# One weight sum of the first MLP set formed by adding DMAs instead of vector adds, in a one-core decoder block

## The chip, the cores and the metric

The kernel runs on one core of one Trainium2 chip. The metric is the device time of one execution in microseconds (us), the median over runs; lower is better. All data is float32.

## What is computed

One decoder block on 512 tokens of width 1024: a mixer, a cross-attention, and a squared-ReLU MLP, each behind an RMSNorm and with a residual add, and a final RMSNorm. The change lies in the first projection of the MLP:

```python
hm = rms_norm(x, g_mlp[l])
x = x + jnp.square(jax.nn.relu(hm @ w_up[l])) @ w_down[l]   # w_up 1024 x 4096, w_down 4096 x 1024
return rms_norm(x, g_final)
```

## The kernel before

**Tiling.** Everything stands transposed: features on the 128 partitions, 512 tokens along the free axis. A product of float32 matrices is made of three matmuls (`mm3`, lines 105 to 107): both operands are split into a rounded high part (a cast on ACT, line 111) and a low remainder (a subtraction on DVE, line 112), and hi·hi, hi·lo and lo·hi are summed in PSUM. A weight block is a tile of 128 x 1024; it is loaded to `wraw` (3 buffers) or `mraw` (5 buffers), split into `whi`/`wlo` (3 buffers each) or, for two of five blocks of the MLP, into two tiles of `mhl` (4 buffers), and consumed by TensorE in the order in which the program lists the blocks.

**The up projection.** It is done in 8 sets of 512 output features, two sets for each of 4 groups, each followed by that group's 8 down blocks. A set multiplies a 2 x 2 arrangement of weight blocks A11, A12, A21, A22 with a 2 x 2 arrangement of the normed input by seven block products instead of eight: three of them use A11, A12 and A22, and four use sums of blocks, s1 = A22 + A21, s3 = A21 + A11, s2 = s1 + A11 and s4 = s2 + A12. The right factors of the seven (B11, T1, B21, T2, T3, T4, B22) are sums of scaled residual tiles, made once in `right_factors` and `right_rest` (lines 756 to 796). In the first set the order is A11, s1, A12, s2, s3, A22, s4, in the others A11, A12, s1, s2, s3, A22, s4.

**How sums are formed.** `load` (line 155) fetches s1 and s3: a plain DMA of the first block on SP's queue into an `mraw` tile, then a DMA of the second block on POOL's queue that adds to the tile (line 164). s2 and s4 have no load: `combined` (line 175) adds A11, and later A12, in place into the tile of s1 with a DVE add (line 179). So the tile of s1 holds s1, then s2, then s4, and A11 and A12 stay in their buffers until they have been added.

**Order.** `weights` (line 205) is called before each block product: it loads the blocks up to seven ahead and prepares (combines and splits) those up to four ahead. TensorE's order is that of the program (manual schedule). The order on ACT, DVE, POOL and SP is written when the program is built, by a list scheduler with a timeline model of its own; on the chip each of these engines runs its list in order, and a waiting instruction holds all behind it. The tiles of `mraw` and `mhl` take the memory of an earlier pool and exist only from `renew` on, inside the projection before the MLP (`co`, the output projection of the cross-attention, 8 blocks in the order 0, 4, 1, 5, 2, 6, 3, 7). Its last block is consumed directly before A11 of the first set. When a `co` block m is done, `done_co` adds the residual (line 572), and makes the right factors of feature block m: for m < 4 two scaled copies on ACT (lines 764, 765), a difference on DVE (line 766) and the split into a `mix` tile, which is B11 and T1 of that block; for m of 4 to 7 the other factors.

```python
RIGHT = {"A11": "B11", "s2": "T2", "s1": "T1", "s3": "T3", "A12": "B21", "A22": "T4", "s4": "B22"}
def block_product(w, rhs, o):
    for i in range(2):
        for k in range(4):
            e = slice((4 * i + k) * P, (4 * i + k + 1) * P)
            mm3(o[:, i * M:(i + 1) * M], w[0][:, e], w[1][:, e], *rhs[k], k == 0, k == 3)
```

Of the kernel before, what the change touches and what calls it, by code (L numbers as in the profile page):

```python
# [14 lines left out]
ALU = mybir.AluOpType  # L15
# [35 lines left out]
def block_kernel(ctx: ExitStack, tc: tile.TileContext, x0g, xT, memT, wv, wm, wst, wckv, wpool, vecs, csts, outT):  # L51
    nc = tc.nc
# [9 lines left out]
            name=nc.get_next_instruction_name(), act_func_set_id=6, ins=[], outs=[],  # L62
# [13 lines left out]
    def sb(tag, shape, bufs, dt=F32):  # L76
        p = apool if tag in EARLY_TAGS else late["pool"] if tag in LATE_TAGS else pool
        return p.tile(shape, dt, tag=tag, name=nm(tag), bufs=bufs)
# [16 lines left out]
    def f(ap):  # L95
        return ap.bitcast(F32)
# [13 lines left out]
    def split(hi, lo, src, eng=V):  # L110
        S.copy(hi, src)  # L111
        eng.tensor_tensor(lo, src, f(hi), op=ALU.subtract)  # L112
# [25 lines left out]
    blocks = []  # L138
# [5 lines left out]
    raw, ready = {}, {}  # L144

    def fetch(key, src, tag, bufs):
        if key not in raw:
            raw[key] = sb(tag, [P, D], bufs)
            nc.sync.dma_start(raw[key], src)
        return raw[key]  # L150

    def part(n, name):
        return wst[4 * n + PARTS.index(name)]

    def load(i):
        if i >= len(blocks):
            return
        if isinstance(blocks[i], tuple):
            n, name = blocks[i]
            if name in ("s1", "s3"):  # L160
                first, then = ("A22", "A21") if name == "s1" else ("A21", "A11")
                if (n, name) not in raw:
                    r = fetch((n, name), part(n, first), "mraw", 5)
                    nc.gpsimd.dma_start(r, part(n, then), accum_op=ALU.add)  # L164
            elif name in PARTS:
                fetch((n, name), part(n, name), "mraw" if name == "A11" else "wraw", 5 if name == "A11" else 3)
        elif i < 2 and i not in raw:
            r = raw[i] = sb("wraw", [P, D], 3)
            nc.sync.dma_start(r[:, :T], blocks[i][:, :T])
            load_x(2 * i + 1)  # L170
            nc.sync.dma_start(r[:, T:], blocks[i][:, T:])
        else:
            fetch(i, blocks[i], "wraw", 3)

    def combined(n, name):

        if name in ("s2", "s4"):
            r = raw[n, "s1"]
            V.tensor_tensor(r, r, raw[n, "A11" if name == "s2" else "A12"], op=ALU.add)
            return r  # L180
        return raw[n, name]

    def prep(i):
        if i >= len(blocks) or i in ready:
            return
        load(i)
        r = combined(*blocks[i]) if isinstance(blocks[i], tuple) else raw[i]
        if i >= FIRST_UP and i % 5 > 2:
            hi = sb("mhl", [P, D], 4, F32R)
            lo = sb("mhl", [P, D], 4, F32R)  # L190
        else:
            hi = sb("whi", [P, D], 3, F32R)
            lo = sb("wlo", [P, D], 3, F32R)
        if i == 0:
            V.tensor_copy(hi[:, :T], r[:, :T])
            V.tensor_tensor(lo[:, :T], r[:, :T], f(hi[:, :T]), op=ALU.subtract)
            split(hi[:, T:], lo[:, T:], r[:, T:])
        elif i == 1:
            for c in (slice(T), slice(T, D)):
                split(hi[:, c], lo[:, c], r[:, c])  # L200
        else:
            split(hi, lo, r, G if i in WPOOL else V)
        ready[i] = (hi, lo)

    def weights(i):
        far = 4 if i >= FIRST_UP else 0
        for j in range(i, i + 4 + far):
            if j < FIRST_UP or late:
                load(j)
        for j in range(i, i + 3 + far // 2):  # L210
            if j < FIRST_UP or late:
                prep(j)
        return ready.pop(i)
# [123 lines left out]
    def load_x(k):  # L337
        xr[k] = tmp()
        nc.sync.dma_start(xr[k], xT[:, k, :])

    def x_in(k):
        pr = pair("xg", 8)
        scaled(pr[:, 0, :], pr[:, 1, :], xr[k], vec[:, G_MIX + k:G_MIX + k + 1])
        xg[k] = (pr[:, 0, :], pr[:, 1, :])

    load(0)
    x_in(0)
    prep(0)
    x_in(1)
    load_x(2)  # L350
# [679 lines left out]
```

## Time and profile before

| | us |
|---|---|
| median of 3 runs (lowest to highest) | 723.29 (722.18 to 724.42) |
| the profiled execution, its own time | 722.57 |
| its span in the profile | 720.8 |
| TensorE busy in the span | 706.5 (98%) |
| VectorE (DVE) / ScalarE (ACT) busy | 510.6 (71%) / 392.5 (54%) |

The profile is of one execution. The span runs from its first to its last instruction; 1.8 us of its own time lie around it. All times in the rows below are us from the span's start, durations of single instructions by group are ns where it says so. An idle time in brackets names what released the engine; where an engine waited for several things, the last is named. SP and POOL issue DMAs: q1 is the queue of the plain loads issued on SP, q0 that of the adding loads issued on POOL. TensorE's granted clock was 1.00 in every stretch up to 620 us.

### The profile page before, as it was taken

The page shows a single profiled execution, that of the slowest core. Times are in us where ns is not written, and L with a number is a line of the kernel's source. Part 1 is how long each engine was busy: PE and PEld are TensorE (multiplying, and loading weights), DVE is VectorE, ACT ScalarE, POOL GpSimd, SP SyncE. Part 2 cuts the span into 40 slices and gives each one's busy share as a digit, 9 for nine tenths or more (in the row PEclk, how much of TensorE's full clock was granted, in tenths as well). Part 3 has the DMA queues.
Part 4 walks back from the last instruction along what each step waited for, and adds up shares of the span by engine and source line. Part 5 has one row for each costly group of instructions (what it writes and reads, how often), then busy time and mean ns, then how long its engine had stood idle before and what let it go on. Part 6 is the DMA issues. An engine that isn't in the chain of part 4 may idle for free.

```text
span 720.8 us, 10378 instructions
## 1 busy us (share of the span) xinstructions
PE 706.5 (98%) x4016; PEld 617.0 (86%) x4016; DVE 510.6 (71%) x797; ACT 392.5 (54%) x646; POOL 66.9 (9%) x59
## 2 busy tenths in 40 slices
PE   8999999999999999999999999999999999999995
PEld 6887888788889888888879988999889988899894
DVE  7698999975888546572999954598446973589525
ACT  7498998676766434452865641355214641256432
POOL 0044112534000000000000000000000000000000
PEclk9999999999999999999999999999999999999999
DMA  8443223143525552113924850558216661305103
GB/s 315 151 118 116 88 75 116 60 146 119 176 88 176 181 170 83 65 58 143 246 79 127 237 164 30 150 111 294 89 33 167 205 182 58 88 30 161 45 1 116
DMA packets 28257, 91.09 MB, mean 126 GB/s; under 512 B 3089, under 2 KB 5137, under 8 KB 28209
## 3 DMA queue, kind: packets, MB, share of 16 engines
q1 hardware_dynamic: 25856, 81.92, 33.5%
q0 software_dynamic: 2352, 8.52, 7.0%
q8 instruction: 31, 0.51, 0.3%
q14 instruction: 18, 0.14, 0.1%
HBM read 86.24 MB, written 2.10 MB: 123 GB/s over the span
## 4 chain that ended last, share of the span: by engine, by line
PE 89%; DVE 5%; ACT 4%; issue 1%; DMA 0%; POOL 0%; DVEq 0%; SPq 0%; ACTq 0%
PE acc L105 17%; PE acc L106 17%; PE acc L107 17%; PE sc L105 11%; PE sc L106 11%; PE sc L107 11%; ACT tmp L447 1%; PE sc L386 1%; PE sc L388 1%; PE sc L390 1%; DVE tmp L445 1%; DVE wlo L112 1%; ACT tmp L417 1%; ACT whi L111 1%; DMA wraw<-wv 0%
## 5 line engine op out<-in xcount | busy, mean ns | idle before, releaser
L111 ACT CAST whi<-wraw 128x1024 fp32r<-128x1024 f32 (+1 forms) x94 | 97.2, 1035 | 107.5 <-PE acc L106 41.0
L105 PE MATMUL acc<-xg,whi 128*128 128x512 f32 x392 | 155.0, 395 | 0.0
L107 PE MATMUL acc<-xg,wlo 128*128 128x512 f32 x392 | 153.0, 390 | 0.0
L106 PE MATMUL acc<-xg,whi 128*128 128x512 f32 x392 | 152.7, 390 | 0.0
L112 DVE TENSOR_TENSOR wlo<-wraw,whi 128x1024 fp32r<-128x1024 f32 (+1 forms) x94 | 115.1, 1226 | 26.8 <-ACT whi L111 26.4
L107 PEld LDWEIGHTS acc<-xg,wlo 128*128 128x128 f32 x392 | 73.6, 188 | 15.8
L105 PEld LDWEIGHTS acc<-xg,whi 128*128 128x128 f32 x392 | 73.7, 188 | 14.5
L106 PEld LDWEIGHTS acc<-xg,whi 128*128 128x128 f32 x392 | 73.7, 188 | 14.3
L572 DVE TENSOR_TENSOR vr<-acc,vr 128x512 f32<-128x512 f32 x39 | 26.9, 690 | 76.5 <-PE acc L107 76.4
L105 PE MATMUL sc<-mix,whi 128*128 128x256 f32 (+1 forms) x184 | 54.2, 295 | 0.0
L107 PE MATMUL sc<-mix,wlo 128*128 128x256 f32 (+1 forms) x184 | 54.1, 294 | 0.0
L106 PE MATMUL sc<-mix,whi 128*128 128x256 f32 (+1 forms) x184 | 54.0, 294 | 0.0
L164 POOL DMA_DIRECT2D mraw<-wst x16 | 13.8, 864 | 429.1 <-DMA mraw<-wst 302.3
L111 ACT CAST whi<-mraw 128x1024 fp32r<-128x1024 f32 x24 | 25.0, 1052 | 45.9 <-PE acc L106 33.0
L890 DVE TENSOR_TENSOR tmp<-sc,tmp 128x512 f32<-128x512 f32 x56 | 37.5, 684 | 6.5 <-PE sc L107 6.4
L111 ACT CAST mhl<-wraw 128x1024 fp32r<-128x1024 f32 x19 | 20.0, 1052 | 34.4 <-PE acc L106 18.0
L106 PE MATMUL acc<-xg,mhl 128*128 128x512 f32 x96 | 37.4, 390 | 0.0
L105 PE MATMUL acc<-xg,mhl 128*128 128x512 f32 x96 | 37.4, 389 | 0.0
L107 PE MATMUL acc<-xg,mhl 128*128 128x512 f32 x96 | 37.4, 389 | 0.0
L107 PEld LDWEIGHTS sc<-mix,wlo 128*128 128x128 f32 x184 | 34.5, 188 | 1.1
L105 PEld LDWEIGHTS sc<-mix,whi 128*128 128x128 f32 x184 | 34.6, 188 | 1.0
L106 PEld LDWEIGHTS sc<-mix,whi 128*128 128x128 f32 x184 | 34.5, 187 | 1.1
(274 smaller groups left out, 1731.4 us busy)
## 6 DMA issues: line engine op xcount, KB each, us to landing
wraw<-wm SPq DMA_DIRECT2D x76, 512.0 KB, 3.5
mraw<-wst SPq DMA_DIRECT2D x24, 512.0 KB, 3.9
wraw<-wckv SPq DMA_DIRECT2D x16, 512.0 KB, 3.4
mraw<-wst POOLq DMA_DIRECT2D x16, 512.0 KB, 6.1
wraw<-wst SPq DMA_DIRECT2D x16, 512.0 KB, 3.4
s<-s SPq DMA_DIRECT2D x8, 256.0 KB, 3.7
vr<-xT SPq DMA_DIRECT2D x8, 256.0 KB, 4.5
outT<-mix SPq DMA_DIRECT2D x8, 256.0 KB, 2.4
```

The source lines that it names most:

```text
L105: nc.tensor.matmul(o, lh, rh, start=start, stop=False)
L106: nc.tensor.matmul(o, lh, rl, start=False, stop=False)
L107: nc.tensor.matmul(o, ll, rh, start=False, stop=stop)
L111: S.copy(hi, src)
L112: eng.tensor_tensor(lo, src, f(hi), op=ALU.subtract)
L164: nc.gpsimd.dma_start(r, part(n, then), accum_op=ALU.add)
L386: nc.tensor.matmul(o[i], xg[k][0][:, tb], wh[:, c], start=k == 0, stop=False)
L388: nc.tensor.matmul(o[i], xg[k][1][:, tb], wh[:, c], start=False, stop=False)
L390: nc.tensor.matmul(o[i], xg[k][0][:, tb], wl[:, c], start=False, stop=k == KC - 1)
L417: S.copy(b[32 * (j ^ 1):32 * (j ^ 1) + 32, :], o[32 * j:32 * j + 32, :])
L572: V.tensor_tensor(t, o, t, op=ALU.add)
L890: V.tensor_tensor(u[new], o, u[old], op=ALU.add)
```

## The change

For the first set alone (n = 0), s2 gets an `mraw` tile of its own, loaded together with s1: a plain DMA of A22, then an adding DMA of A21 and an adding DMA of A11. `combined` returns this tile for s2 and for s4 without an add. Right behind the split of s2 a third adding DMA puts A12 into the same tile, which makes it s4. The two DVE adds of line 179 are gone for this set; the other seven sets are as they were, and `mraw` keeps its five buffers.

```diff
@@ load
                 if (n, name) not in raw:
                     r = fetch((n, name), part(n, first), "mraw", 5)
                     nc.gpsimd.dma_start(r, part(n, then), accum_op=ALU.add)
+                if (n, name) == (0, "s1") and (n, "s2") not in raw:
+                    r = fetch((n, "s2"), part(n, first), "mraw", 5)
+                    for then in "A21", "A11":
+                        nc.gpsimd.dma_start(r, part(n, then), accum_op=ALU.add)
@@ combined
+        if name in ("s2", "s4") and n == 0:
+            return raw[n, "s2"]
         if name in ("s2", "s4"):
             r = raw[n, "s1"]
             V.tensor_tensor(r, r, raw[n, "A11" if name == "s2" else "A12"], op=ALU.add)
@@ prep
         ready[i] = (hi, lo)
+        if blocks[i] == (0, "s2"):
+            nc.gpsimd.dma_start(r, part(0, "A12"), accum_op=ALU.add)
```

## Rows read from the trace of the kernel before

**Rows 1.** The page, busy time in us, share of the span, instructions, by engine (DVE is VectorE, ACT is ScalarE).
```profile
PE 706.5 (98%) x4016; PEld 617.0 (86%) x4016; DVE 510.6 (71%) x797; ACT 392.5 (54%) x646; POOL 66.9 (9%) x59
```

**Rows 2.** Busy time of each engine by stretch: the stretch, its length, busy us and instructions of each engine, TensorE's granted clock, the DMA engines' mean busy share, GB/s. The first set's sums are loaded and split from 334 to 390.
```profile
345.00:360.00 15.00, 15.00 (x68) 12.43 (x67) 14.97 (x25) 12.81 (x22) 0.86 (x1) 1.00 0.91 258
360.00:370.00 10.00, 10.00 (x46) 8.29 (x45) 10.00 (x18) 6.43 (x12) 0.00 (x0) 1.00 0.50 142
370.00:380.00 10.00, 8.68 (x58) 7.72 (x57) 9.19 (x15) 7.79 (x13) 0.00 (x0) 1.00 0.12 34
420.00:520.00 100.00, 100.00 (x603) 89.42 (x602) 61.95 (x72) 36.81 (x45) 3.45 (x4) 1.00 0.46 138
620.00:721.00 101.00, 92.35 (x639) 85.90 (x637) 63.13 (x86) 42.80 (x64) 0.86 (x1) 0.98 0.24 74
```

**Rows 3.** What TensorE waited for from 325 to 420: us in total, times, the longest.
```profile
PE sc L106 <- DVE mix L112: 1.0, 1, 1.0
PE sc L105 <- ACT mix L111: 0.4, 1, 0.4
```

**Rows 4.** TensorE in order of time around the first set: start, us, engine, line, operation, out<-in, idle before. `mhl` and `whi` name the weight block's kind: the first matmul of A11 (373.10), the two behind its idle times, and the first matmuls of s1, s3 and s4.
```profile
373.10 0.28 PE L105 MATMUL sc<-mix,mhl 128*128 128x256 f32 x1
...
374.04 0.28 PE L107 MATMUL sc<-mix,mhl 128*128 128x256 f32 x1
374.69 0.39 PE L105 MATMUL sc<-mix,mhl 128*128 128x256 f32 x1 [0.37 <-ACT mix L111]
376.03 0.39 PE L106 MATMUL sc<-mix,mhl 128*128 128x256 f32 x1 [0.96 <-DVE mix L112]
...
377.79 0.28 PE L105 MATMUL sc<-mix,whi 128*128 128x256 f32 x1
...
386.73 0.28 PE L105 MATMUL sc<-s,mhl 128*128 128x256 f32 x1
...
392.38 0.28 PE L105 MATMUL sc<-mix,whi 128*128 128x256 f32 x1
```

**Rows 5.** ACT in order of time, the same columns: the casts of s3 (348.88), of s2 (373.07), of the last B11 factor (374.02), of s4 (380.69) and of A11 of the second set (383.98).
```profile
348.88 1.05 ACT L111 CAST mhl<-mraw 128x1024 fp32r<-128x1024 f32 x1 [0.83 <-DMA mraw<-wst]
...
373.07 1.05 ACT L111 CAST whi<-mraw 128x1024 fp32r<-128x1024 f32 x1 [1.25 <-PE acc L106]
374.02 0.61 ACT L111 CAST mix<-tmp 128x512 fp32r<-128x512 f32 x1
...
380.69 1.05 ACT L111 CAST whi<-mraw 128x1024 fp32r<-128x1024 f32 x1 [0.57 <-PE sc L106]
...
383.98 1.05 ACT L111 CAST whi<-mraw 128x1024 fp32r<-128x1024 f32 x1 [1.93 <-PE sc L106]
```

**Rows 6.** DVE in order of time, the same columns. L179 are the two adds of the first set, s2 at 366.28 and s4 at 376.56.
```profile
349.96 1.22 DVE L112 TENSOR_TENSOR mhl<-mraw,mhl 128x1024 fp32r<-128x1024 f32 x1
...
366.28 1.22 DVE L179 TENSOR_TENSOR mraw<-mraw,mraw 128x1024 f32<-128x1024 f32 x1
367.42 0.68 DVE L112 TENSOR_TENSOR mix<-tmp,mix 128x512 fp32r<-128x512 f32 x1
...
371.29 0.42 DVE L766 TENSOR_TENSOR tmp<-tmp,tmp 128x256 f32<-128x256 f32 x1
...
372.23 0.42 DVE L112 TENSOR_TENSOR s<-tmp,s 128x256 fp32r<-128x256 f32 x1
373.30 0.69 DVE L572 TENSOR_TENSOR vr<-acc,vr 128x512 f32<-128x512 f32 x1 [0.65 <-PE acc L107]
374.15 1.22 DVE L112 TENSOR_TENSOR wlo<-mraw,whi 128x1024 fp32r<-128x1024 f32 x1 [0.16 <-ACT whi L111]
375.29 0.68 DVE L112 TENSOR_TENSOR mix<-tmp,mix 128x512 fp32r<-128x512 f32 x1
...
376.56 1.22 DVE L179 TENSOR_TENSOR mraw<-mraw,wraw 128x1024 f32<-128x1024 f32 x1
377.70 0.68 DVE L112 TENSOR_TENSOR mix<-tmp,mix 128x512 fp32r<-128x512 f32 x1
```

**Rows 7.** SP's queue in order of time: start, from the first to the last issue, count.
```profile
334.54 2.33 SPq L149 DMA_DIRECT2D mraw<-wst  x5
345.49 2.99 SPq L149 DMA_DIRECT2D wraw<-wm  x2
```

**Rows 8.** The DMA issue of SP between 345 and 346, the last `co` block but one: KB, and us from issue to landing.
```profile
wraw<-wm SPq DMA_DIRECT2D x1, 512.0 KB, 7.6
```

**Rows 9.** POOL's queue in order of time: the adding DMAs of s1, s3 and of s1 of the second set.
```profile
339.76 0.88 POOL L164 DMA_DIRECT2D mraw<-wst  x1 [160.46 <-DMA mraw<-wst]
340.99 0.86 POOL L164 DMA_DIRECT2D mraw<-wst  x1 [0.34 <-DMA mraw<-wst]
344.09 0.86 POOL L164 DMA_DIRECT2D mraw<-wst  x1 [2.25 <-DMA mraw<-wst]
```

**Rows 10.** What the DMA queues moved from 343 to 348: packets, MB, share of the 16 engines. Adding loads (q0) run almost alone.
```profile
q0 software_dynamic: 260, 0.98, 104.9%
```

**Rows 11.** The same from 352 to 355: plain loads (q1) run almost alone.
```profile
q1 hardware_dynamic: 342, 1.24, 101.2%
```

**Rows 12.** All sixteen adding DMAs of line 164: ns min/median/max of the issue on POOL, and us from issue to landing.
```profile
L164 POOL DMA_DIRECT2D mraw<-wst x16: 862/862/880, 339.8 to 621.3; - x16
DMA to landing us min/median/max: 5.2/6.1/9.5
```

## The prediction

> **What bounds the kernel now.** I first read the page's busy times: TensorE is busy for 706.5 of 720.8 us [rows 1], so 14.3 us at most are to be had, and only where TensorE stands still. The busy times by stretch say where. From 620 to the end 8.65 us are idle, the tail, which the change does not touch; from 420 to 520 nothing is [rows 2]. Near the sums of the first set one hole is left, 1.32 us between 370 and 380, and there DVE is full: 14.97 of 15 us from 345 to 360 and 10.00 of 10 from 360 to 370 [rows 2]. TensorE's waits give the hole two owners, a cast on ACT and a remainder on DVE, both writing a `mix` tile, a right factor, and neither a weight [rows 3].
>
> In order of time A11 starts at 373.10, stops behind 374.04 for the cast of the last B11 factor, again until 376.03 for its remainder, and s1 starts at 377.79 [rows 4]. A block product is 24 matmuls; s3 and A22 together take 392.38 - 386.73 = 5.65 us [rows 4], so one takes 2.82. A11 took 377.79 - 373.10 = 4.69: the hole costs **1.87 us**. Nothing behind it stops TensorE again near by, so what is won or lost here should reach the end in full.
>
> Why is the factor late? Its difference is done on DVE at 371.29 + 0.42 = 371.71 [rows 6]. ACT could cast it then, but the next instruction in ACT's list is the cast of s2, which idles 1.25 us for the last `co` block to release its `whi` buffer and starts at 373.07; the factor's cast follows at 374.02 [rows 5]. On DVE the remainder of s2 (374.15) stands likewise ahead of the factor's remainder (375.29) [rows 6]. So at the hole two lists have s2 ahead of the factor, and what opens the jam is the release of a buffer by TensorE, not the sum that the change moves.
>
> **The change, part by part.** *The add of s2* at 366.28 goes: the next instruction started 1.14 us later [rows 6], so DVE's list moves up 1.14 us from there. But DVE already idles 0.65 us at 373.30 for the `co` block and 0.16 at 374.15 for ACT's cast [rows 6]: both wait for TensorE, so with the lists as they are, s2's cast stays at 373.07, the factor's remainder at 375.29, the hole at 1.87 us. Worth on the path: **0**; in reserve: 1.14 + 0.81 = 1.95 us by which DVE may be later than it would be without the add before the hole grows.
>
> *The add of s4* at 376.56 (1.14 us to 377.70 [rows 6]) lies behind the hole, where TensorE waits for nothing: **0**.
>
> *The plain load of A22* takes one of the five places that SP fills at 334.54 [rows 7]. What it pushes out is s1 of the second set, which now waits until A11 is split and its buffer free; it is consumed only after s4 of the first set, beyond 392.38 + 2.82 = 395.2 [rows 4]. **0**; a plain load costs the DMA engines 0.524 MB / (1.24 MB in 3 us) = 1.27 us [rows 11].
>
> *The two adding DMAs of s2.* Each costs POOL 0.86 us, in a list that idles, and the DMA engines 0.524 / (0.98 MB in 5 us) = **2.68 us** [rows 10, 12]. They chain: s2's second waits for its first to land. s2 itself is cast at 373.07, over 30 us after the first issues at 339.76 [rows 5, 9], room for both with the longest landing, 2 x 9.5 us [rows 12]. What is late next is what stands behind them. (a) The add of s3 was second in POOL's list (340.99 [rows 9]); it becomes third, behind one of s2's, so lands 2.68 us later, and 3.95 if the pushed-out load of 1.27 us shares the engines with it. ACT's cast of s3 already waited 0.83 us for that landing, at 348.88, and DVE's remainder stands at 349.96 in a list with no gap [rows 5, 6, 2]. If the lists keep that cast where it is, ACT and DVE start everything behind it B = 0 to 3.95 us later, and the hole grows by B - 1.95: 0 up to **+2.0**, +0.7 at 2.68. I take **0**: a cast that waited just 0.83 us shows a list that follows the landings closely, and s3 is not consumed until 386.73 [rows 4], so its cast can move behind the later landing. (b) The two plain loads issued from 345.49 are for the last two `co` blocks; the first landed 7.6 us on, at 353.1 [rows 7, 8]. A `co` block has 24 matmuls twice as wide, some 5.65 us (estimated from the pair above), so that one is consumed from about 373.10 - 11.3 = 361.8: two more adds (5.4 us) fit in those 8.7 us. **0**.
>
> *The third adding DMA*, A12 into s2's tile, cannot issue before s2's remainder is read at 374.15 + 1.22 = 375.37 [rows 6]. The DMA engines are at 0.12 there [rows 2]; at 5.2 to 6.1 us to landing [rows 12] s4 is there at 380.6 to 381.5. Its cast starts at 380.69 now, and the cast behind it idles 1.93 us before 383.98 [rows 5], which hides up to that; even at 9.5 us (384.9) cast and remainder (1.05 + 1.22) end at 387.2, before s4 is consumed at 392.38 [rows 4, 5, 6]. **0**.
>
> **Sum:** 0, bounds -1.87 (the hole closed) and +2.0. Against the profiled execution that is 722.57; it lies 0.72 below the median of the runs, and it is the median that I predict: **723.3 us**.
>
> **Rivals.** *The lists change and the hole closes.* With DVE 1.14 us earlier the factor's difference ends at 370.57, 2.5 us before s2's cast can start. The list on ACT is written anew; if it puts the factor's cast ahead, cast (0.61) and remainder (0.68) are done before 373.1 and 1.87 us are won: **721.4**. For it: the idle 1.25 us on ACT. Against it: the factor was ready 1.36 us ahead of s2's cast already and the list did not use that.
>
> *Slower: s3's add stands behind both of s2's in POOL's list.* Place: POOL, which would wait for s2's first add to land (about 348.9, when s3's second-in-line add landed) before it issues the second, and s3's after that. s3 then lands some 5.2 + 2.7 us later, B = 7.9, and if its cast keeps its place in ACT's list the hole grows by 7.9 - 1.95 = 6.0: **729.3**. It counts as slower than the 2.2 us (0.3%, about what a measurement of this kernel can tell from no change) from B = 4.1 on. For it: the program names s2's adds before s3's. Against it: s3's add needs only its own plain load, which lands well before s2's first add does.
>
> *Adds that start late beside a full DVE.* Landing times of adds spread from 5.2 to 9.5 us [rows 12]; were s3's add slowed by that whole spread, B = 4.3 and the hole grows by 2.35: **725.6**. The Trainium skill, "SBUF — State Buffer", section "SBUF: two separate sides", has a rule that would work so: while DVE runs an operation in its two-port mode, POOL cannot write the descriptors of the DMAs that it issues, so a DMA on POOL's queue waits for DVE; its example, in the section "A bandwidth-pool intuition that's wrong (but worth ruling out)", is 620 ns alone against 3100 beside a DVE copy. By that rule three more adds on POOL would be three more such waits, here beside a DVE that never rests. This trace does not bear it out: the issue took 862 to 880 ns in all sixteen adds [rows 12], those beside a full DVE included, so I give it little.
>
> **How the numbers follow.** Forecast (lists kept, B from 0 to 3.95, 723.3 to 725.3) 0.50; hole closed, wholly or in part, 0.30; s3 behind both adds 0.15; late adds 0.05. The range 721.0 to 726.5 holds the first two and the last, and leaves out the slow rival (0.15) and little else; the forecast's own range is 722.8 to 725.3. Faster by over 2.2 us needs the closed hole and a third of a microsecond of luck: about a third of 0.30, 0.11. Slower: the slow rival and a little of the late adds, 0.16. The same: 0.73.
>
> **What would show it.** After the change DVE should have no add between the differences before 371 and be idle for about 1.8 us before 373.3; TensorE's two waits for `mix` should still stand at A11, 1.9 us together; s2's cast should start as TensorE releases its buffer; s4's cast should start within about 1 us of now. The forecast is wrong if the factor's cast stands ahead of s2's on ACT (fast), if ACT idles 4 us or more for s3's landing near 350 (slow), or if s4's cast holds the next set's.

## The result: 725.12 us against 723.18, and where the time went

Nine runs of each: 725.12 us (724.36 to 726.89) with the change, 723.18 us (722.18 to 725.01) before. The ratio is 1.0029, 95% interval 1.0018 to 1.004: the change is slower by some 2 us. The execution profiled after the change took 725.12 us, with a span of 723.4.

The two profiles stand 0.26 us apart already before the first instruction that differs, so I measure from a common point, the last matmuls of the attention output, among the first `co` blocks (331.51 us before, 331.77 after), and cut TensorE's time at first matmuls: A11, s1, s2, s3, the first down block, and the final norm's sum (the stretch from s1 to s2 holds A12 and the sum of squares of the MLP's norm). Differences to the kernel before in us, one profiled execution each; the runs' ratio stands beside it.

| kernel | to A11 | A11 | s1 to s2 | s2 to s3 | s3 to down | down to end | sum | ratio of runs (95%) |
|---|---|---|---|---|---|---|---|---|
| before (us) | 41.59 | 4.69 | 6.11 | 2.83 | 28.26 | 295.53 | 379.01 | |
| the change | +1.63 | -1.56 | +0.01 | +0.80 | +0.44 | +0.46 | +1.78 | 1.0029 (1.0018-1.004) |
| e1 no third DMA | +1.89 | -1.58 | +1.39 | 0.00 | +0.01 | -0.01 | +1.70 | 1.002 (1.0011-1.0029) |
| e2 third DMA only | 0.00 | +0.01 | -0.03 | -0.11 | -0.53 | +0.45 | -0.21 | 0.9999 (0.9989-1.001) |
| e3 s2 behind s3 | +0.41 | -1.57 | -0.02 | +1.24 | +0.44 | +0.43 | +0.93 | 1.0015 (1.0005-1.0026) |
| e4 no adds at all | -0.01 | -1.86 | -0.01 | -0.12 | -0.53 | +0.64 | -1.89 | 0.9979 (0.997-0.9987) |
| e5 behind, no third | -0.01 | -1.86 | +1.13 | 0.00 | 0.00 | +0.01 | -0.73 | 0.9993 (0.9984-1.0002) |
| e6 s3's cast late | +0.96 | -0.10 | -0.02 | +2.44 | +0.07 | +0.02 | +3.37 | 1.0057 (1.0043-1.007) |
| e7 s2 on POOL | 0.00 | -1.61 | +1.41 | -0.01 | +0.01 | 0.00 | -0.20 | 0.9996 (0.9987-1.0005) |
| e8 both moves | +1.18 | -0.16 | +1.79 | 0.00 | 0.00 | 0.00 | +2.81 | 1.0049 (1.0032-1.0066) |
| e10 POOL and third | 0.00 | -0.94 | +0.01 | +1.80 | +0.45 | +0.41 | +1.73 | 1.0002 (0.9988-1.0015) |
| e11 POOL both | 0.00 | -0.48 | +1.35 | -0.01 | +0.01 | 0.00 | +0.87 | 0.9999 (0.9989-1.0009) |
| e12 behind, s4 on POOL | 0.00 | -1.72 | +1.34 | 0.00 | 0.00 | +0.03 | -0.35 | 1.0004 (0.9995-1.0013) |
| e13 s4 in its own tile | 0.00 | -1.61 | +0.01 | -0.01 | +0.01 | -0.03 | -1.63 | 0.9988 (0.9979-0.9997) |

(Sums of a single profile and ratios of runs agree to a few tenths of a per cent, no better: e10's profile is slower than its runs.)

The change's row holds the story: 1.63 us lost before A11, the hole of A11 closed (-1.56), then 0.80 lost at s3 and 0.90 behind it. TensorE's busy time by stretch after the change, answering to [rows 2]:

```profile
345.00:360.00 15.00, 15.00 (x68) 12.40 (x67) 11.03 (x17) 9.78 (x16) 1.73 (x2) 1.00 1.05 256
360.00:370.00 10.00, 8.62 (x38) 6.86 (x37) 10.00 (x19) 8.08 (x15) 0.86 (x1) 1.00 0.79 218
370.00:380.00 10.00, 9.97 (x63) 8.90 (x62) 10.00 (x19) 7.94 (x13) 0.86 (x1) 1.00 0.48 135
380.00:390.00 10.00, 9.36 (x78) 9.07 (x77) 7.54 (x11) 6.30 (x10) 0.00 (x0) 1.00 0.59 156
```

The idle time has moved from 370:380 to 360:370 and 380:390, and DVE, full before in 345:360 (14.97), stood still for 4 us there (11.03). TensorE's waits from 325 to the end, after, answering to [rows 3]:

```profile
PE acc L105 <- DVE vr L580: 1.4, 1, 1.4
PE sc L105 <- DVE tmp L898: 0.6, 1, 0.6
PE acc L106 <- DVE xg L112: 0.2, 1, 0.2
```

The first is a `co` block waiting for one of the two `acc` buffers of PSUM, which DVE's residual add frees; the second is s3 waiting for a `sc` buffer that DVE's add of a block product frees; the third a down block waiting for an activation. The two waits for `mix` are gone. TensorE in order of time (the `co` block, A11, s1, s3), answering to [rows 4]:

```profile
364.02 0.47 PE L105 MATMUL acc<-xg,whi 128*128 128x512 f32 x1 [1.38 <-DVE vr L580]
...
374.99 0.28 PE L105 MATMUL sc<-mix,mhl 128*128 128x256 f32 x1
...
378.12 0.28 PE L105 MATMUL sc<-mix,whi 128*128 128x256 f32 x1
...
387.87 0.39 PE L105 MATMUL sc<-s,mhl 128*128 128x256 f32 x1 [0.64 <-DVE tmp L898]
```

Why DVE stood still is on ACT (s3's cast at 356.42, the last B11 factor, s2, s4; answering to [rows 5]; the last line is A11 of the second set) and in DVE's remainders of s3, s2 and s4 (second fence; answering to [rows 6]):

```profile
356.42 1.05 ACT L111 CAST mhl<-mraw 128x1024 fp32r<-128x1024 f32 x1 [5.22 <-DMA mraw<-wst]
...
374.80 0.62 ACT L111 CAST mix<-tmp 128x512 fp32r<-128x512 f32 x1
375.33 1.04 ACT L111 CAST whi<-mraw 128x1024 fp32r<-128x1024 f32 x1
...
383.97 1.05 ACT L111 CAST whi<-mraw 128x1024 fp32r<-128x1024 f32 x1 [2.66 <-DMA mraw<-wst]
...
385.23 1.04 ACT L111 CAST whi<-mraw 128x1024 fp32r<-128x1024 f32 x1
```

```profile
357.50 1.23 DVE L112 TENSOR_TENSOR mhl<-mraw,mhl 128x1024 fp32r<-128x1024 f32 x1 [3.97 <-ACT mhl L111]
...
376.83 1.21 DVE L112 TENSOR_TENSOR wlo<-mraw,whi 128x1024 fp32r<-128x1024 f32 x1
...
385.05 1.23 DVE L112 TENSOR_TENSOR wlo<-mraw,whi 128x1024 fp32r<-128x1024 f32 x1 [2.46 <-ACT whi L111]
```

ACT waits 5.22 us for s3's landing and DVE 3.97 behind it. The factor's cast (374.80) now stands ahead of s2's (375.33): the list was written the other way round, and the hole is closed. At the end ACT waits 2.66 us for s4, DVE 2.46 behind it, and in DVE's list the add that s3's product needs stands behind s4's remainder. POOL's queue (the adds of s1, s2 first, s3, s1 of the second set, s2 second, s3 of the second set, and the third DMA, s4), answering to [rows 9]:

```profile
340.03 0.88 POOL L164 DMA_DIRECT2D mraw<-wst  x1 [160.43 <-DMA mraw<-wst]
342.33 0.86 POOL L168 DMA_DIRECT2D mraw<-wst  x1 [1.42 <-DMA mraw<-wst]
343.54 0.86 POOL L164 DMA_DIRECT2D mraw<-wst  x1 [0.35 <-DMA mraw<-wst]
349.66 0.86 POOL L164 DMA_DIRECT2D mraw<-wst  x1 [5.25 <-DVE wlo L112]
352.92 0.86 POOL L168 DMA_DIRECT2D mraw<-wst  x1 [2.39 <-DMA mraw<-wst]
365.96 0.86 POOL L164 DMA_DIRECT2D mraw<-wst  x1 [12.19 <-DVE s L112]
378.33 0.86 POOL L211 DMA_DIRECT2D mraw<-wst  x1 [11.51 <-DVE wlo L112]
```

s3's add is third, as the prediction had it, and issues at 343.54. It lands 12.9 us later; the DMA issue of that stretch, and what the two queues moved from 350 to 360:

```profile
mraw<-wst POOLq DMA_DIRECT2D x1, 512.0 KB, 12.9
```

```profile
q0 software_dynamic: 378, 1.36, 68.1%
q1 hardware_dynamic: 375, 1.41, 37.2%
```

Packet for packet the queues share the DMA engines (378 against 375), and an adding packet takes nearly twice a plain one's time. The Trainium skill, "DMA: Bandwidth & Descriptors", section "SWDGE vs HWDGE vs iDMA", says that inside a DMA engine the two kinds of queues are served in turn; from 350 on this trace agrees. From 346 to 349 it does not: a plain load issued at 345.75 stood, with hardly a packet moved, while the adds ran:

```profile
q0 software_dynamic: 165, 0.61, 102.6%
q1 hardware_dynamic: 6, 0.02, 1.9%
```

### The profile page after: what moved, and what is told of

The parts are those of the page before. It is cut to its first block, busy times and chain, and to the rows that moved or that the text cites. A ratio compares the mean times of both kernels' runs of the same rounds, so it can differ in the third digit from the quotient of the medians.

```text
span 723.4 us, 10386 instructions
## 1 busy us (share of the span) xinstructions
PE 707.6 (98%) x4016; PEld 616.9 (85%) x4016; DVE 507.8 (70%) x795; ACT 392.4 (54%) x646; POOL 69.4 (10%) x62
## 4 chain that ended last, share of the span: by engine, by line
PE 77%; DVE 10%; ACT 5%; DMA 5%; issue 2%; POOL 0%; DVEq 0%; SPq 0%; ACTq 0%
PE acc L105 15%; PE acc L106 15%; PE acc L107 15%; PE sc L105 9%; PE sc L107 9%; PE sc L106 8%; DMA mraw<-wst 3%; DVE wlo L112 2%; ACT tmp L455 1%; ACT whi L111 1%; PE sc L394 1%; DVE tmp L898 1%; DVE mix L112 1%; PE sc L396 1%; PE sc L398 1%
```

## The experiments

Each ran beside the kernel before on the same chip. **One part at a time.** e1 takes the third DMA away, e2 keeps it alone, e3 moves s2's DMAs behind s3's, e4 leaves out the adds.

e1, s4 by a DVE add in s2's own tile:

```diff
         if name in ("s2", "s4") and n == 0:
-            return raw[n, "s2"]
+            r = raw[n, "s2"]
+            if name == "s4":
+                V.tensor_tensor(r, r, raw[n, "A12"], op=ALU.add)
+            return r
...
-        if blocks[i] == (0, "s2"):
-            nc.gpsimd.dma_start(r, part(0, "A12"), accum_op=ALU.add)
```

> The change without its third adding DMA: s2 still comes from two adding DMAs into a tile of its own, but s4 is made by a DVE add of A12 into that tile, as before the change. Main theory (two causes: s3's add lands late and stalls ACT near 350, which costs TensorE about 1.6 us in the last co blocks and is paid back by the closed hole at A11; and s4's cast waits for the third DMA, which costs 0.8 us at s3 and about 0.9 us behind it): 725.1 - 1.7 = 723.4 us, TensorE's wait for a DVE add of line 890's kind near 387 gone, ACT's wait for s3's landing still 5 us. Rival A (the third DMA costs nothing, all of the loss is from s3's late add): 725.1 us. Rival B (all of the net loss and more is from the third DMA): below 722.5 us.

Measured: 724.13 us against 722.89, ratio 1.002. The expected 723.4 was too low and rival B fails. Rival A's 725.1 lies just above the interval (723.7 to 725.0), too near to fall by the time alone, but the profile is not the one it wants. The wait at s3 is gone, ACT's wait for s3 stays (5.5 us), but a new wait of TensorE comes in its place, for the split of the norm's sum of squares:

```profile
PE acc L105 <- DVE vr L581: 1.6, 1, 1.6
PE tr L244 <- DVE tmp L112: 1.1, 1, 1.1
```

With the hole at A11 closed the norm is due earlier, and s4's add stands ahead of its split in DVE's list.

e2, s2 by the DVE add as before, s4 by the third DMA:

```diff
-                if (n, name) == (0, "s1") and (n, "s2") not in raw:
-                    r = fetch((n, "s2"), part(n, first), "mraw", 5)
-                    for then in "A21", "A11":
-                        nc.gpsimd.dma_start(r, part(n, then), accum_op=ALU.add)
...
-        if name in ("s2", "s4") and n == 0:
-            return raw[n, "s2"]
+        if name == "s4" and n == 0:
+            return raw[n, "s1"]
```

> The third adding DMA alone: s2 is a DVE add into s1's tile as in the kernel before, and only A12 is added to it by a DMA behind the split of s2. Main theory: s3's add lands as before (cast near 349, wait about 0.8 us), the hole of 1.87 us at A11 stays, and s4's cast waits 2 to 3 us for the DMA: 723.2 + 0.8 to 1.7 = 724.0 to 724.9 us. Rival A (the third DMA costs nothing): 723.2 us.

Measured: 722.68 us against 722.89, ratio 0.9999: rival A, and a miss of the main theory. The DMA issued at 375.48, s4's cast waited 0.73 us for it and TensorE not at all; the hole of A11 stays open, and with it the slack that hides the wait.

```profile
380.77 1.05 ACT L111 CAST whi<-mraw 128x1024 fp32r<-128x1024 f32 x1 [0.73 <-DMA mraw<-wst]
```

e3, s2's fetch and adds under s3's instead of s1's:

```diff
-                if (n, name) == (0, "s1") and (n, "s2") not in raw:
-                    r = fetch((n, "s2"), part(n, first), "mraw", 5)
+                if (n, name) == (0, "s3") and (n, "s2") not in raw:
+                    r = fetch((n, "s2"), part(n, "A22"), "mraw", 5)
```

> The whole change, with the load and the two adding DMAs of s2 placed behind those of s3, so that s3's add is second on POOL again. Main theory: s3's add lands within 3 us of where it did before, ACT's wait near 350 falls from 5.2 to under 2 us, TensorE's wait for DVE's residual in the last co blocks (1.4 us) goes; the third DMA still costs its 0.8 to 1.7 us: 725.1 - 1.6 = 723.5 us. Rival C (the added DMA traffic as such delays the loads, wherever the adds stand): 725.1 us, with the wait of 1.4 us still there.

Measured: 724.41 us against 722.89, ratio 1.0015. The loss before A11 falls from 1.63 to 0.41, as the main theory wants and rival C does not; ACT's wait falls to 3.63 us, not under 2, and the time is 0.9 us above the expected 723.5. The third DMA now costs more, 1.24 at s3:

```profile
352.59 1.05 ACT L111 CAST mhl<-mraw 128x1024 fp32r<-128x1024 f32 x1 [3.63 <-DMA mraw<-wst]
```

```profile
PE sc L105 <- DVE tmp L898: 1.2, 1, 1.2
```

e4, the plain load and the tile kept, the three adding DMAs left out, so that s2 and s4 of this set are A22 alone:

```diff
-                    for then in "A21", "A11":
-                        nc.gpsimd.dma_start(r, part(n, then), accum_op=ALU.add)
...
-        if blocks[i] == (0, "s2"):
-            nc.gpsimd.dma_start(r, part(0, "A12"), accum_op=ALU.add)
```

> The change with all three adding DMAs of s2's tile left out: the tile holds A22 alone for s2 and s4 of the first set, so the up projection of that set is computed with other weights; the plain load, the fifth tile and the two missing DVE adds are as in the change. Main theory: no late landing, no wait for s4, and the hole at A11 closed in whole or in part because DVE is 1.14 us earlier and the factor's cast stands ahead of s2's: 723.2 - 1.2 to 1.9 = 721.3 to 722.0 us. Rival D (the hole closed after the change only because ACT was late, and nothing is to be won by the missing adds): 723.2 us.

Measured: 721.51 us against 722.89, ratio 0.9979: the main theory. Freeing DVE of both adds is worth the whole hole, 1.86 us, when nothing is put in their place. So rival D falls: the hole did not close after the change only because ACT was late.

**Remedies.** e5 is e3 and e1 together (both diffs):

> s2's load and two adding DMAs placed behind those of s3, and no third DMA: s4 is a DVE add of A12 into s2's tile. Main theory (the loss is the sum of s3's late landing and of the third DMA behind a late DVE): the pieces measured apart add up, +0.4 us before A11 and -1.6 at A11, nothing behind: 722.9 - 1.2 = 721.7 us. Rival E (with the DVE add back in its list, the sum of squares is again late for the norm, as in the run without the third DMA, where TensorE waited 1.1 us for it): 723 us or more.

Measured: 722.67 us against 722.76, ratio 0.9993 (0.9984 to 1.0002), no difference that can be told. Nothing is lost before A11 and the hole is closed in full, but rival E took 1.13 of its 1.86 us back:

```profile
PE tr L244 <- DVE tmp L112: 0.9, 1, 0.9
```

The add is not all that stands ahead of the norm's split (`tmp<-ss,tmp`). In e1, e5 and e7 DVE's list has s4's remainder (`wlo`), too, ahead of it, where the kernel before has it behind. Before, and in e5:

```profile
380.98 0.68 DVE L112 TENSOR_TENSOR tmp<-ss,tmp 128x512 fp32r<-128x512 f32 x1
381.78 1.22 DVE L112 TENSOR_TENSOR wlo<-mraw,whi 128x1024 fp32r<-128x1024 f32 x1
```

```profile
380.55 1.23 DVE L112 TENSOR_TENSOR wlo<-mraw,whi 128x1024 fp32r<-128x1024 f32 x1
381.68 0.69 DVE L112 TENSOR_TENSOR tmp<-ss,tmp 128x512 fp32r<-128x512 f32 x1
```

What each of the two costs was not tried apart.

e6 swaps the buffers of s3 and s4 in the first set:

```diff
-        if i >= FIRST_UP and i % 5 > 2:
+        if i >= FIRST_UP and (i % 5 > 2) != (blocks[i] in ((0, "s3"), (0, "s4"))):
```

> The whole change as it is, all DMAs in the same places, but in the first set s3 is split into the whi and wlo buffers and s4 into mhl, where it was the other way round. s3's cast then has to wait for a whi buffer that is released after s1, near 379, so it can't stand on ACT near 350. Main theory (it is the cast's place in ACT's list that turns the late landing into a loss): ACT's wait of 5 us near 356 goes, A11 starts no later than before the change, the hole at A11 stays closed, the third DMA costs between nothing and 1.7 us: 721.3 to 723.0 us. Rival C (the traffic itself delays what TensorE needs): 724.5 us or more, with the wait for DVE's residual still there.

Measured: 727.41 us against 722.76, ratio 1.0057. The expectation failed, and the way it failed is instructive: with `mhl` free of s3, the list put the cast of A22, the next block in `mhl`, into the early place, where it waited for A22's plain load, late behind the adds:

```profile
364.82 1.05 ACT L111 CAST mhl<-wraw 128x1024 fp32r<-128x1024 f32 x1 [4.89 <-DMA wraw<-wst]
```

So e6 does not tell the cast's place from the traffic, as it was meant to: rival C's time came, though the early cast that waited is the main theory's mechanism. The loss before A11 and the open hole go with it; the larger part, 2.4 us, is a wait at s3 for the same DVE add as in the change, behind the third DMA, which issued at 379.52. e8 adds the same swap to e5:

> Both remedies: s2's load and two adds behind those of s3, s3 in whi and s4 in mhl, and s4 made by a DVE add. Main theory: neither s3's landing nor a third DMA holds anything: 722.9 - 1.4 to 1.9 = 721.0 to 721.5 us. Rival C (traffic): 722.5 us or more.

Measured: 727.26 us against 722.76, ratio 1.0049, with the same kind of wait, 4.99 us; a miss for the same reason. It has no third DMA and no wait at s3, and lost 1.8 us at the norm.

e7 adds no DMA and gives the one add of s2 to POOL:

```diff
-            V.tensor_tensor(r, r, raw[n, "A11" if name == "s2" else "A12"], op=ALU.add)
+            eng = G if (n, name) == (0, "s2") else V
+            eng.tensor_tensor(r, r, raw[n, "A11" if name == "s2" else "A12"], op=ALU.add)
```

> The kernel before, with the one add of s2 of the first set moved from DVE to POOL; no DMA is added, s4 stays a DVE add. Main theory (relief of DVE by 1.14 us puts the factor's cast ahead of s2's on ACT and is worth the hole): hole at A11 under 0.4 us, 722.9 - 1.4 to 1.9 = 721.0 to 721.5 us. Rival F (POOL's add slows DVE beside it or ends after s2's cast could start, so the gain is lost): 722.5 us or more.

Measured: 722.93 us against 722.76, ratio 0.9996. The hole closes (-1.61) and the norm takes 1.41 back, as in e5, so the time is rival F's, but not by its road: POOL's add ended before s2's cast, and although it slowed DVE, the hole closed. The add on POOL, and the DVE remainder that it held up:

```profile
365.31 5.59 POOL L180 TENSOR_TENSOR mraw<-mraw,mraw 128x1024 f32<-128x1024 f32 x1 [7.04 <-DVE wlo L112]
```

```profile
369.16 2.83 DVE L112 TENSOR_TENSOR wlo<-wraw,whi 128x1024 fp32r<-128x1024 f32 x1
```

That remainder takes 1.22 us elsewhere. e10 is e7 with s4 by the third DMA as in e2; e12 is e5 with s4's add on POOL; e11 gives POOL both adds of the kernel before:

```diff
-            V.tensor_tensor(r, r, raw[n, "A11" if name == "s2" else "A12"], op=ALU.add)
+            eng = G if n == 0 else V
+            eng.tensor_tensor(r, r, raw[n, "A11" if name == "s2" else "A12"], op=ALU.add)
```

> Kernel before with s2's add on POOL (as in the run before, where POOL took 5.6 us for it) and s4 by the third adding DMA alone; no DVE add and no extra load in the crowded stretch near 345. Main theory (the closed hole is only kept if nothing stands ahead of the norm's sum of squares on DVE, and s3's cast is on time): A11 without its hole (-1.6 to -1.9), no wait of TensorE for the norm's split (1.1 us with s4's add on DVE), s4's cast waits 1 to 3 us for its DMA and costs 0 to 0.8 us: 722.8 - 0.8 to 1.9 = 720.9 to 722.0 us. Rival G (the third DMA costs as much as the add that it replaces): 722.5 us or more, with a wait of over 1 us at s3.

> Both adds of the first set, s2's and s4's, on POOL; no DMA is added to the kernel before. Main theory: as in the run with POOL and the third DMA: 720.9 to 722.0 us. Rival H (POOL's second add takes 5 us or more beside a full DVE, s4's cast is late and holds DVE's adds of the block products as the third DMA did): 722.5 us or more, with a wait of TensorE for a DVE add near 387.

> s2 by two adding DMAs that stand behind those of s3, and s4's add of A12 on POOL. Main theory: the hole at A11 closed (-1.9), no DVE add ahead of the norm's sum of squares, s4's cast 0 to 3 us late: 722.8 - 0.8 to 1.9 = 720.9 to 722.0 us. Rival H (s4 on POOL as late as the third DMA was): 722.5 us or more.

Measured: 723.17, 722.99 and 723.24 us against 722.62, ratios 1.0002, 0.9999 and 1.0004, all without a difference that can be told, and all above what the main theory expected. e10 has 1.6 us of wait at s3 (rival G), and in e10 and e11 a part of the hole stayed open as well (0.9 and 1.4 us), though ACT's list has the factor ahead of s2 in both. In e11 and e12 s4 on POOL took 4.06 us and cost the norm as much as DVE's own add, since a DVE remainder beside it took 3.4 us (below, e12); so rival H has the time, but the wait is at the norm and not at s3:

```profile
377.38 3.44 DVE L112 TENSOR_TENSOR mhl<-wraw,mhl 128x1024 fp32r<-128x1024 f32 x1
```

e13 gives s4 a tile of its own too, loaded behind s2's in e3's place, without a DMA behind the split of s2, so that its adds wait for no split:

```diff
+                if (n, name) == (0, "s3") and (n, "s4") not in raw:
+                    r = fetch((n, "s4"), part(n, "A22"), "mraw", 5)
+                    for then in "A21", "A11", "A12":
+                        nc.gpsimd.dma_start(r, part(n, then), accum_op=ALU.add)
...
         if name in ("s2", "s4") and n == 0:
-            return raw[n, "s2"]
+            return raw[n, name]
```

> s2 and s4 of the first set each in a tile of its own, loaded behind s3: s2 by two, s4 by three adding DMAs, none of which waits for a split; no DVE add. Main theory (a closed hole is kept if neither a DVE add stands ahead of the norm's sum of squares nor s4 waits for the split of s2): A11 and the norm without waits of TensorE, s4's cast not held by its landing: 722.7 - 1.2 to 1.9 = 720.8 to 721.5 us. Rival C (five adds of 2.7 us each in the stretch from 342 to 375 delay the plain loads of the last co blocks, of A12 and A22, and with them ACT and DVE): 722.7 us or more, with TensorE waiting before A11.

Measured: 721.68 us against 722.70, ratio 0.9988 (0.9979 to 0.9997): a little faster than the kernel before, and 0.2 us above the expected range. It moves more by DMA than the change does, also from 345 to 360, where the change lost its time (277 GB/s against 256), and TensorE has no wait in the stretch:

```profile
345.00:360.00 15.00, 15.00 (x68) 12.43 (x67) 12.72 (x22) 11.83 (x20) 1.56 (x2) 1.00 1.05 277
360.00:370.00 10.00, 10.00 (x46) 8.27 (x45) 10.00 (x18) 6.88 (x12) 1.92 (x3) 1.00 0.96 259
370.00:380.00 10.00, 10.00 (x73) 9.30 (x73) 10.00 (x18) 8.62 (x14) 0.86 (x1) 1.00 1.00 218
380.00:390.00 10.00, 10.00 (x86) 9.92 (x85) 9.23 (x14) 6.02 (x10) 0.86 (x1) 1.00 0.65 181
```

The DMA engines are full from 370 to 380 (share 1.00), and it costs nothing. So the volume of the added traffic alone is not what made the change slow: what counts is which landing an engine's list waits for. ACT's wait for s3 is still there, 3.17 us, and costs nothing:

```profile
351.41 1.05 ACT L111 CAST mhl<-mraw 128x1024 fp32r<-128x1024 f32 x1 [3.17 <-DMA mraw<-wst]
```

## The prediction, step by step

The forecast was no measurable change, 723.3 us, with an upper bound of +2.0 us. The measured +1.94 us lies just under that bound, and below the 2.2 us taken as the least that can be told; with nine runs of each kernel the interval still shows it as a loss. So the time came out within the range, but not by the working: a gain of 1.56 us that the forecast did not count on and three losses set to 0 happen to leave +1.8, and that is luck. All three signs that were to show the forecast wrong are in the trace: the factor's cast ahead of s2's on ACT, 5.22 us of ACT's idle time for s3's landing, and the cast of A11 of the second set, which had 1.93 us of idle time before it, close behind s4's late cast (385.23).

**What bounds the kernel** held: a hole of 1.87 us at A11, made by two lists that had s2 ahead of the factor. e4 got 1.86 of it.

**The add of s2, 0 on the path.** Wrong, in the direction of the first rival. With DVE relieved the list on ACT was written anew with the factor ahead of s2, and the hole closed: -1.56 in the change, -1.6 to -1.9 in e1, e3, e4, e5, e7, e12 and e13, which have the add of s2 off DVE. It closed in part in e10 and e11 (-0.94 and -0.48), with that add on POOL, and hardly in e6 and e8, where ACT and DVE were late. In e2, with that add in place, the hole stays. The rival's argument against itself, that the list had not used a gap of 1.36 us, carried no weight.

**The adds of s2 in front of s3's, taken as B = 0.** This is the step that failed. The bound for the landing's shift was 3.95 us; it was 356.42 - 348.88 - 0.26 = 7.3. The runs split it only roughly (one profile each, corrected by its own offset at the common point). Where nothing is loaded beside s3's add that was not before, its cast stands 0.5 to 1.8 us later than in the kernel before (e2, e7, e10, e11), which is how much a landing scatters; with the plain load alone 2.0 (e4); with s2's adds behind s3's 2.3 to 3.3 (e3, e5, e12, e13); with s2's first add ahead of s3's 7.3 and 7.5 (the change and e1). So the place of that one add is worth 4 to 5 us, and the share of the plain load can't be told from the scatter. The working had the adds run at their lone rate of 2.68 us; but the adds start only when the plain loads are through, and from 349.5 on they share the DMA engines with the `co` weights packet by packet. And "a list that follows the landings closely" was a poor ground: the list did move the cast six places back, and ACT still idled 5.22 us there.

**Where that loss shows.** The working let it grow the hole (B - 1.95). It came one step earlier: a late residual add kept an `acc` buffer, and TensorE stood 1.38 us in the `co` blocks. Of the 4 us that DVE stood still only 1.63 reached TensorE. By the working's own rule a shift of 7.3 us would have grown the hole by 5.3. The runs show how much the lists absorb: 2.7 to 3.2 us of ACT's idle time for s3 cost nothing before A11 (e5, e12, e13), 3.6 cost 0.41 (e3), 5.2 cost 1.63 (the change), 5.5 cost 1.89 (e1), so some 3.2 to 3.6 us, and not the 1.95 of the working, are free.

**The third DMA, 0.** Right with the hole open (e2), wrong with it closed. It was worked out from an issue at 375.4; DVE was late, it issued at 378.33 and landed 5.6 us on, within the 5.2 to 6.1 used. The 1.93 us of ACT's idle time that were to cover it, and all of the slack up to s3, belonged to a TensorE that lost 1.87 us at A11: once that was won back, the cover was gone. That is one of two differences: in e2 the DMA issued at 375.48, in e3 and e10 at 377.25 and 377.40, and no run has the hole closed and the early issue. It cost 0.80 in the change, 1.24 in e3 and 1.80 in e10. Some 0.9 us follow behind s3 in these three. Half of it is no wait: a few block products ran at 0.122 to 0.127 us a matmul where the kernel before has 0.118. The 0.2 us wait of a down block for an activation stands in their traces and not in those of e1, e5, e7, e11, e12 and e13, where nothing is lost there. It stands in e2 and e4 as well, where it takes back what a faster pace had won. That the late s4 causes it in the change is argued, not shown.

**The add of s4, 0 because it lies behind the hole.** True before, and false once the hole is closed: e1, e5 and e7 lose 1.1 to 1.4 us at the norm with it (and with s4's remainder moved ahead of the norm's split), and e4 and e13, without it on DVE or POOL and with s4 on time, lose nothing there.

**The rivals.** The slow one, s3's add behind both of s2's on POOL, did not come; one of them was enough. Adds held by a full DVE did not show either: the issues took 0.86 us as before, though s3's add was 12.9 us under way, beyond the 9.5 of that rival.

**The sum** of the change, which the forecast had at 0, is then 1.63 - 1.56 + 0.80 + 0.90 = 1.8 us in the profile, against 1.94 in the runs.

## What to carry to other kernels

A cost hidden by a wait is hidden only as long as that wait stands: when a step is meant to close a hole, work out every term again with the hole closed, since the two adds that were free before it (on DVE for the norm, by DMA for s3) were the next bounds. Where lists are written by a scheduler and run in order, an operand that lands late costs through what stands behind its first reader, so put new transfers behind those that the next reader waits for, and let none of them depend on a split that is itself late. Price a transfer in a crowded stretch with the queue ahead of it and the queue beside it, not at its lone rate.

## What the hardware showed that was not expected

The first adding packets moved 2.7 us after the first adding DMA issued before the change (339.76 to 342.5) and 4.5 after it (340.03 to 344.6), in both cases as the plain loads already queued came to their end; the adds then ran almost alone, beside plain loads already issued, and from 349 on the two queues shared packet by packet. An add of 128x1024 on POOL took 5.6 us for s2 (e7, e10, e11) and 4.06 for s4 (e11, e12), beside a DVE without a gap in each case, and one DVE operation with two SBUF inputs beside it took 2.83 to 3.44 us instead of 1.22. Each time that operation ended 1.1 us after POOL's add did (in e7 at 371.99, POOL at 370.90), as if it ran only once POOL was through; DVE's operations that began earlier beside the same add kept their usual length. The Trainium skill, "SBUF — State Buffer", section "SBUF: two separate sides", has DVE operations with two SBUF inputs and POOL operations that read SBUF share a pair of ports that one of them holds alone; for the operation that was held up these rows agree. Between 384 and 408 the block products of e2 and e4 ran at 0.113 us a matmul, those of the kernel before and e13, and most of the change's, at 0.118, all at a granted clock of 1.00; what sets the pace was not tried.
